# A planned fp32 decoder kernel on one core: norm weights by rows at the layer boundary, one PSUM tile per transpose group, two buffers of transposed probabilities, and a planner with other durations

## The chip, the core and the metric

The kernel runs on one core of one Trainium2 chip. The number that counts is the device time of one execution in microseconds (us). The engines of the core are PE (TensorE, matrix products; its weight loads are listed apart as PEld), DVE (VectorE), ACT (ScalarE), POOL (GpSimd) and SP (SyncE, which here only issues DMAs). Each engine takes its instructions in the order in which they were written, so an instruction that waits holds back all that stand behind it on that engine. SBUF is the on-chip memory, and PSUM is the memory that PE writes and that DVE and ACT read.

## The reference, cut to what is computed

Two layers, 256 tokens, 1024 channels, then a final norm. Each layer reads one normalised input through one wide projection, runs three token mixers on it (a: block attention, which for 256 tokens is plain causal attention; b: attention over the keys that a small indexer selects, 64 for each query; c: attention with a running sum of forget gates as bias), gates each, projects each, merges them by sigmoid gates and adds an output projection to the residual.

```python
def hybrid_layer(x, gain, w_in, f_bias, w_branch, w_out):
    h = rms_norm(x, gain)                      # x * rsqrt(mean(x*x) + eps) * gain
    proj = einsum('bsd,de->bse', h, w_in)      # q,k,v,gate of a, b, c; indexer; forget; merge logits
    oa = moba_attention(rope(qa), rope(ka), va) * silu(ga)
    ob = dsa_attention(rope(qb), rope(kb), vb, rope(qi), rope(ki), wi) * silu(gb)
    log_f = log_sigmoid(f_logit + f_bias)
    oc = forgetting_attention(qc, kc, vc, log_f) * silu(gc)
    y = einsum('nbsw,nwd->bsnd', stack([oa, ob, oc]), w_branch)
    merged = sum(sigmoid(merge_logit) * y, axis=2)
    return x + einsum('bsd,de->bse', merged, w_out)

def reference(x, ...):
    for layer in range(2): x = hybrid_layer(x, ...)
    return rms_norm(x, final_gain)
```

## The kernel before

**Numbers.** Everything is float32. Each operand of a product is split into a high part that PE takes exactly and a low part, the rest (`wh`, `wl` for weights, `hTh`, `hTl` for the normalised input, and so on), and each product is made of three matmuls: high by high, high by low, low by high. A weight goes a fixed way: a DMA brings a piece into one of three `raw` buffers (L373), ACT copies its high part into `wh` (L381), DVE subtracts it and writes `wl` (L385), PE multiplies with both (L429). There are 190 such pieces, and six buffers each of `wh` and `wl`.

**Order.** The Python code writes no instruction directly. It lists operations in a `Plan`: each has the engines that may do it with an assumed duration, what it reads and writes, and a key (a due position, counted in matmul units). `Plan.run` then repeats one step: among the operations that are ready it works out how early each could start by the assumed durations, takes the engine that could start first, and on it the operation of the lowest key among those that can start at that earliest moment. So the assumed durations and keys decide, when the program is built, where each instruction stands in each engine's fixed order, and for some operations which engine does them. On the chip the engines keep these orders and wait for one another by semaphores. `MARGIN` and the like are extra lags that the planner leaves between an operation and a matmul that needs it.

**Units.** A layer's work goes in this order: values of mixer a; the unit `kwf` (the indexer's keys, with the forget logits); the indexer's queries and mixer a, with some merge logits between; mixer c, with merges between; mixer b, with merges between; the rest of the merges; the output projection. In a mixer each pair of heads has projections for queries, gates and keys (units of DVE `ql`, `kl`, rotary steps on DVE and POOL, L488 to L491), scores on PE (L613, 2 heads into a PSUM tile `d`), softmax (DVE L687, ACT L691, DVE L694, then a normalising multiply on DVE L701 or ACT L698), transposes of the probabilities (PE L624), their split (ACT `pth` L716, DVE `ptl` L717, one buffer each), products with the values (PE L729 to L732, in this order the two with `pth`, then the two with `ptl`), and the gate (ACT L745, DVE L747, then a multiply by `g` on POOL L752 or DVE L753). The merge of a branch ends in an add to `acc` (DVE L932 or POOL L933).

**The places around the change.**
- Start and layer boundary use one function, `norm_to_hT`, once per token tile of 128: a sum of squares per half of the channels (ACT L499, at the start also DVE L501), mean (DVE L505), power (POOL L507), a scale by it (ACT L516 for one half, DVE L519 for the other), eight PE transposes (L537) into two `d` tiles, and for each of the eight 128-channel blocks an ACT copy times the gain (`hTh`, L544) and a DVE operation for the rest (`hTl`, L551). The gain lies in `gT`, a channel to a partition, for both layers.
- The forget chain hangs on `wf_cols`: fz (DVE L808 to L816, nine small operations), running sum (PE L822 to L824), its copies (DVE L827, L828), a transposed copy written to DRAM (`drow`, L837) and read back to all partitions (`brow`, L839, two DMAs), from which mixer c makes its bias `fb` (DVE L672). It is listed right behind `kwf`.
- The indexer's selection: eight rounds of MAX8 (L890) and MATCH_REPLACE8 (L891) on DVE, then the mask `selb` (L894, L896). Mixer b needs it.
- Each `d` tile counts in the planner as two banks (`Buf.banks`), so that ACT may work on one half and DVE on the other.
- The merged rows are transposed by token tile (PE L941), both tiles into one `d`, and split (ACT L946, DVE L947).
- At the end of the last layer the final gain is loaded by rows into `acc[:, 0]`, which is free by then.

Of the kernel before, what the change touches and what calls it, by code (L numbers as in the profile page):

```python
# [109 lines left out]

class Plan:
# [38 lines left out]
    def run(self, slack):  # L150
# [4 lines left out]
        while ready:  # L155
# [84 lines left out]
def t_pool(n):  # L240
    return 250.0 + 2.2 * n
# [7 lines left out]
def hybrid_trunk(ctx, tc, x, norm_gain, w_in, forget_bias, w_branch, w_out, final_gain, consts, out):  # L249
# [51 lines left out]
    gT = pool.tile([128, L, KC], F32, name="gT")  # L301
# [8 lines left out]
    pts = [pool.tile([128, 2, 384], F32R, name=f"pt{p}") for p in "hl"]  # L310
# [20 lines left out]
    k_id, k_rope, k_gT, k_cst, k_fb, k_wf, k_widx, k_lf, k_cs, k_csT, k_main = (Tok() for _ in range(11))  # L331
# [18 lines left out]
    plan.tag("pth", pts[:1])  # L350
    plan.tag("ptl", pts[1:])
# [12 lines left out]
    def piece(key, ckey, ap, cshape, sel, shape, k):  # L364
# [21 lines left out]
        act(hi, a * b, False, [c], [p[0]], k - SPLIT_LEAD, f"hi {key}", 18.0)  # L386
        dve(lo, a * b, [c, p[0]], [p[1]], k - SPLIT_LEAD, f"lo {key}", port=True)
# [123 lines left out]
    def scaled(i, src, t, reads, key):  # L511

        r = small[:, t, 3:4]
        o = tmp6[:, i * HD:(i + 1) * HD]
        if i == 0:
            act(lambda: ACT.activation(o, src, AF.Copy, scale=r), HD, False, reads + [k_ss[t][2]], [k_tmp[i]], key,  # L516
                "norm", 93.0)
        else:
            dve(lambda: DVE.tensor_scalar(o, src, r, None, op0=ALU.mult), HD, reads + [k_ss[t][2]], [k_tmp[i]], key,  # L519
                "norm", t_dve2(HD) + 61.0)  # L520
        return o

    def norm_to_hT(l, t, key):
        for i in range(2):
            sum_sq(t, i, key, l == 0)
        rstd(t, key)
        for i in range(2):
            scaled(i, xs[t][:, i * HD:(i + 1) * HD], t, [k_x[t][i]], key)
        dd = [Buf("d"), Buf("d")]
        for b in range(4):  # L530
            ps, at = Tok(), [dd[b // 2], dd[b // 2].banks[b % 2]]
            at_cols = lambda k, d=dd[b // 2], b=b: T(d)[:, b % 2 * 512 + k * 128:b % 2 * 512 + (k + 1) * 128]

# [5 lines left out]
            for k in range(2):
                c = b * 2 + k  # L540
                sl = (slice(None), c, slice(t * 128, (t + 1) * 128))
                src = lambda at_cols=at_cols, k=k: at_cols(k)
                g = gT[:, l, c:c + 1]
                act(lambda sl=sl, src=src, g=g: ACT.activation(hTh[sl], src(), AF.Copy, scale=g), 128, True,  # L544
                    [ps, k_gT], [k_hT[0][t][c]], key, "hT", 93.0, touch=at)
            for k in range(2):
                c = b * 2 + k
                sl = (slice(None), c, slice(t * 128, (t + 1) * 128))
                src = lambda at_cols=at_cols, k=k: at_cols(k)
                g = gT[:, l, c:c + 1]  # L550
                dve(lambda sl=sl, src=src, g=g: DVE.scalar_tensor_tensor(  # L551
                    hTl[sl], src(), g, hTh[sl].bitcast(F32), op0=ALU.mult, op1=ALU.subtract), 128,
                    [ps, k_gT, k_hT[0][t][c]], [k_hT[1][t][c]], key, "hT", t_dve(128) + 61.0, touch=at)
# [74 lines left out]
    class Pair:  # L628
# [49 lines left out]
        def softmax(self, d, key):  # L678
            bs = [self.bias(h, key) for h in range(2)]
            es, ke = [], []  # L680
            for h in range(2):
# [12 lines left out]
                dve(lambda st=st: DVE.reciprocal(T(st)[:, 4:6], T(st)[:, 2:4]), 2, [], kt, key, "recip", 75.0, touch=[st])  # L694
# [13 lines left out]
        def values(self, ps, key):  # L708
# [25 lines left out]
            pe(av, 696.0, kv + [ph, pl] + [t for h in kp for t in h], [o], key, "av", MARGIN)  # L734
# [4 lines left out]
        def gated(self):  # L739
# [9 lines left out]
            def gate():  # L749
# [3 lines left out]
                     ("DVE", t_dve(S), lambda: DVE.tensor_tensor(*gate(), op=ALU.mult))],  # L753
# [29 lines left out]
    def wf_cols(l, key):  # L783
# [15 lines left out]
        dve(pre, 0, [ps, k_fb], [k_lf], key, "lf", 300.0)  # L799

# [348 lines left out]
```

## Time and profile before

Times of the kernel: 599.23, 599.30 and 599.63 us, median 599.3. The profiled execution took 598.98 us, and its span from the first to the last instruction is 597.1 us.

| engine | busy us | share of the span | instructions |
|---|---|---|---|
| PE | 587.2 | 98% | 4332 |
| DVE | 516.8 | 87% | 1164 |
| ACT | 387.0 | 65% | 736 |
| POOL | 100.2 | 17% | 110 |

The page has the time of each engine, a strip of 40 slices, the DMA queues, the chain of work that ended last, and groups of instructions by line and operation. Further views of the trace are used below: PE's waits, grouped by the line waited for; windows, which give each engine's busy time in stretches of the span; groups kept apart by shape; and the timeline, one row for each run of like instructions: start, duration, engine, line, operation, result and operands, and in brackets the idle time of that engine just before, with what ended it. PE pipelines its matmuls, so rows overlap: what a matmul costs is the distance from its start to the next start.

### The profile page before, as it was taken

How to read it: one execution, taken by the hardware profiler on the slowest of the kernel's cores; microseconds unless marked ns; L12 is line 12 of the kernel's file. 1: busy time of each engine (PE TensorE's matmuls, PEld its weight loads, DVE VectorE, ACT ScalarE, POOL GpSimd, SP SyncE). 2: the span in 40 equal slices, each digit the busy share in tenths (PEclk: the TensorE clock that was granted, in tenths of full speed). 3: DMA queues.
4: the chain of work that ended last, by engine and by line, in shares of the span. 5: the costliest groups of instructions: out<-in, count | busy, mean ns of one | idle time of the engine just before them, and what ended most of it. 6: DMA issues, size and time to landing. Idle time of an engine off the chain costs nothing.

```text
span 597.1 us, 11359 instructions
## 1 busy us (share of the span) xinstructions
PE 587.2 (98%) x4332; PEld 538.2 (90%) x4332; DVE 516.8 (87%) x1164; ACT 387.0 (65%) x736; POOL 100.2 (17%) x110
## 2 busy tenths in 40 slices
PE   8999999999999999999999999999999999999995
PEld 7989998989998999888889899898999899998885
DVE  6799999877898989978588999997869898998773
ACT  5767539585677757774487754676748785758441
POOL 1241040200000334200004221320000023440001
PEclk9999999999999999999999999999999999999999
DMA  8849546546464554474546747464574464447411
GB/s 289 278 145 349 176 131 228 181 136 213 140 212 143 155 199 142 145 264 155 164 141 212 249 149 240 142 212 143 176 246 143 141 212 142 143 144 271 150 35 72
DMA packets 75831, 107.59 MB, mean 180 GB/s; under 512 B 4208, under 2 KB 45440, under 8 KB 75776
## 3 DMA queue, kind: packets, MB, share of 16 engines
q1 hardware_dynamic: 75488, 106.47, 54.4%
q8 instruction: 34, 0.56, 0.4%
q10 hardware_dynamic: 288, 0.39, 0.2%
q14 instruction: 21, 0.17, 0.1%
HBM read 105.79 MB, written 1.06 MB: 179 GB/s over the span
## 4 chain that ended last, share of the span: by engine, by line
PE 85%; DVE 10%; issue 2%; ACT 1%; DMA 1%; POOL 0%; POOLq 0%; DVEq 0%
PE proj L429 74%; PE d L613 4%; DVE wl L385 3%; PE proj L1027 2%; PE d L624 2%; PE o L732 1%; PE o L729 1%; DVE isc L891 1%; DVE t L890 1%; PE o L731 1%; PE d L941 1%; DVE rsh L488 1%; DMA x<-in_x_dram 1%; PE o L730 0%; ACT wh L381 0%
## 5 line engine op out<-in xcount | busy, mean ns | idle before, releaser
L385 DVE TENSOR_TENSOR wl<-raw,wh 128x1024 fp32r<-128x1024 f32 (+1 forms) x190 | 235.1, 1250 | 26.3 <-ACT wh L381 23.2
L381 ACT ACTIVATE wh<-raw 128x1024 fp32r<-128x1024 f32 (+1 forms) x190 | 198.2, 1055 | 74.7 <-PE proj L429 37.1
L429 PE MATMUL proj<-hTh,wh 128*128 128x256 f32 (+1 forms) x656 | 155.6, 276 | 0.0
L429 PE MATMUL proj<-hTl,wh 128*128 128x256 f32 (+1 forms) x656 | 154.9, 275 | 0.0
L429 PEld LDWEIGHTS proj<-hTh,wh 128*128 128x128 f32 (+1 forms) x656 | 125.2, 191 | 0.6
L429 PEld LDWEIGHTS proj<-hTl,wh 128*128 128x128 f32 (+1 forms) x656 | 125.2, 191 | 0.3
L429 PE MATMUL proj<-wh,hTh 128*128 128x512 f32 x272 | 105.1, 386 | 0.0
L429 PE MATMUL proj<-wh,hTl 128*128 128x512 f32 x272 | 103.3, 380 | 0.2 <-DVE hTl L551 0.2
L429 PE MATMUL proj<-hTh,wl 128*128 128x256 f32 (+1 forms) x656 | 100.4, 276 | 0.0
L429 PEld LDWEIGHTS proj<-hTh,wl 128*128 128x128 f32 (+1 forms) x656 | 86.2, 191 | 0.2
L429 PE MATMUL proj<-wl,hTh 128*128 128x512 f32 x272 | 81.0, 379 | 0.3 <-DVE wl L385 0.3
L489 POOL TENSOR_TENSOR rsh<-rsh,cst 128x256 f32<-128x256 f32 (+1 forms) x42 | 38.4, 915 | 165.9 <-DVE rsh L488 164.3
L429 PEld LDWEIGHTS proj<-wl,hTh 128*128 128x128 f32 x272 | 51.3, 189 | 7.9 <-DVE wl L385 0.7
L429 PEld LDWEIGHTS proj<-wh,hTl 128*128 128x128 f32 x272 | 51.5, 189 | 7.5 <-DVE hTl L551 1.2
L429 PEld LDWEIGHTS proj<-wh,hTh 128*128 128x128 f32 x272 | 51.4, 189 | 7.5
L691 ACT ACTIVATE e<-e,st 128x128 f32<-128x128 f32 x96 | 42.4, 443 | 22.8 <-DVE st L687 22.5
L491 POOL TENSOR_TENSOR rr<-rr,rsh 128x256 f32<-128x256 f32 (+1 forms) x42 | 41.5, 989 | 12.6 <-DVE rr L490 8.8
L752 POOL TENSOR_TENSOR ot<-ot,g 128x256 f32<-128x256 f32 x10 | 8.1, 814 | 200.6 <-DVE ot L747 129.1
L429 PE MATMUL proj<-wh,v 128*128 128x512 f32 (+1 forms) x144 | 34.0, 359 | 0.0
L429 PEld LDWEIGHTS proj<-wh,v 128*128 128x128 f32 x144 | 25.1, 190 | 2.8
L429 PE MATMUL proj<-wh,og0h 128*128 128x512 f32 x64 | 25.0, 391 | 0.0
L717 DVE TENSOR_TENSOR ptl<-d,pth 128x768 fp32r<-128x768 f32 x24 | 22.9, 953 | 2.2 <-ACT pth L716 1.9
(193 smaller groups left out, 926.8 us busy)
## 6 DMA issues: line engine op xcount, KB each, us to landing
raw<-in_w_in_dram SPq DMA_DIRECT2D x74, 1024.0 KB, 5.2
raw<-in_w_branch_dram SPq DMA_DIRECT2D x12, 1024.0 KB, 5.1
raw<-in_w_out_dram SPq DMA_DIRECT2D x8, 1024.0 KB, 5.1
brow<-drow SPq DMA_DIRECT2D x4, 512.0 KB, 6.6
raw<-in_w_in_dram SPq DMA_DIRECT2D x3, 512.0 KB, 6.2
x<-in_x_dram SPq DMA_DIRECT2D x4, 256.0 KB, 5.5
raw<-in_w_in_dram SPq DMA_DIRECT2D x2, 320.0 KB, 6.2
out_dram<-tmp SPq DMA_DIRECT2D x2, 320.0 KB, 2.5
```

The source lines that it names most:

```text
L381: ACT.activation(p[0].v, sel(c.v), AF.Copy)
L385: DVE.tensor_tensor(p[1].v, sel(c.v), p[0].v.bitcast(F32), op=ALU.subtract)
L429: PE.matmul(o(), a(), b(), start=first and i == 0, stop=last and i == n - 1)
L488: dve(lambda: DVE.stream_shuffle(T(sh)[:np_], a(), SWAP), S, [ps], [sh], key, "rope", t_dve(S) + 6.0)
L489: gps(lambda: POOL.tensor_tensor(T(sh)[:np_], T(sh)[:np_], s[:np_], op=ALU.mult), S, [k_rope], [sh], key, "rope")
L491: gps(lambda: POOL.tensor_tensor(T(r)[:np_], T(r)[:np_], T(sh)[:np_], op=ALU.add), S, [sh], [r], key, "rope")
L613: PE.matmul(T(d)[:, c:c + n].rearrange("p (b a) -> p b a", a=2), st[r, sl], turns(mv[r, :n]), start=i == 0, stop=i == 2, skip_group_check= ...
L624: PE.matmul(T(d)[:, u * 512 + j * 64:u * 512 + j * 64 + 64], e[r], ident[r, r], is_transpose=True, start=True, stop=True, skip_group_check ...
L691: act(lambda t=t, a=a, n=n, e=e, st=st: ACT.activation(T(e)[:, a:a + n], T(e)[:, a:a + n], AF.Exp, bias=T(st)[:, t:t + 1], scale=-1.0, acc ...
L717: dve(lambda src=src, dst=dst: DVE.tensor_tensor(dst(pl), src(), dst(ph).bitcast(F32), op=ALU.subtract), 128 * n, [ps, k[0]], k[1:], key, ...
L752: plan.op([("POOL", t_pool(S), lambda: POOL.tensor_tensor(*gate(), op=ALU.mult)), ("DVE", t_dve(S), lambda: DVE.tensor_tensor(*gate(), op= ...
L1027: PE.matmul(T(ps[t]).rearrange("p (b a) -> p b a", a=2), h(2 * i + x, t), turns(v3(w)[:, x]), start=left[t][0] == 23, stop=left[t][0] == 0)
```

## The change

The parts, with the names of the diff:

1. **Start.** `norm_to_hT` is now `first_hT` for layer 0. Its transposes go into four PSUM tiles for each token tile, two transposes to a tile, by `GROUPS` (for the first token tile `d`, `proj`, `d`, `proj`), in place of halves of two `d` tiles. `gT` holds the gain of layer 0 alone. The second token tile's input comes by one DMA.
2. **Boundary.** The new `norm_to_hT` has the gain of layer 1 loaded by rows into `acc[:, 0]` ("next gain", 512 KB, as the final gain was already). One DVE operation per half multiplies x by the power and the gain; four PE transposes go to one `d` tile; ACT copies 512 wide and DVE subtracts 512 wide, where there were four operations each. The sum of squares may be on DVE here too. Its DVE and POOL operations have a `rush` of 400 ns: the planner may take them though something else could start up to 400 ns sooner. Their keys are 10 and 8 units ahead instead of 2.
3. **PSUM tiles.** A `d` tile is one bank to the planner (`[Bank()] * 2`), and the merged rows have a `d` tile for each token tile.
4. **Probabilities.** Two buffers each of `pth` and `ptl` (`pt0h`, `pt1h`, `pt0l`, `pt1l`).
5. **Forget chain.** `wf_cols` stops after the first two small operations; the rest is a function `forget`, which is listed after the units of mixer a, with a later key.
6. **Durations.** The planner's assumed times: POOL 320 instead of 250 ns as the fixed part, split copies +42 and +54 ns, `split_to` 90 and 110, a gate's split 100, the gate on DVE +80, reciprocal 91; the lag ahead of the products with the values 600 instead of `MARGIN` (200), ahead of the half-row products 300.
7. ACT's first table is asked for at the start by a Tanh on `half`.

```diff
-        self.no, self.last, self.banks = None, None, [Bank(), Bank()]
+        self.no, self.last, self.banks = None, None, [Bank()] * 2
...
-            e = min(best, key=best.get)
+            e = min(cand, key=lambda c: c[0] - c[3].rush)[4][0]
             lim = best[e] + slack.get(e, 0.0)
-            t, _, _, o, w = min((c for c in cand if c[4][0] == e and c[0] <= lim), key=lambda c: (c[1], c[2]))
+            t, _, _, o, w = min((c for c in cand if c[4][0] == e and c[0] <= lim + c[3].rush), key=lambda c: (c[1], c[2]))
...
 def t_pool(n):
-    return 250.0 + 2.2 * n
+    return 320.0 + 2.2 * n
...
-    pts = [pool.tile([128, 2, 384], F32R, name=f"pt{p}") for p in "hl"]
+    pts = [pool.tile([128, 2, 384], F32R, name=f"pt{i}{p}") for p in "hl" for i in range(2)]
...
+    def norm_to_hT(l, t, key):
+        a = len(plan.ops)
+        for i in range(2):
+            sum_sq(t, i, key, True)
+        r = rstd(t, key)
+        for i in range(2):
+            c = slice(i * HD, (i + 1) * HD)
+            x, o = xs[t][:, c], tmp6[:, c]
+            d = Buf("d")
+            dve(lambda x=x, o=o, c=c: DVE.scalar_tensor_tensor(o, x, r, acc[:, 0, c], op0=ALU.mult, op1=ALU.mult), HD,
+                [k_x[t][i], k_ss[t][2], k_fg, k_acc[0][0], k_acc[1][0]], [k_tmp[i]], key, "norm")
+            at, kt, ks4 = [d, d.banks[0]], Tok(), slice(4 * i, 4 * i + 4)
...
+            act(lambda h=h, src=src: ACT.activation(h, src(), AF.Copy), HD, True, [kt], k_hT[0][t][ks4], key, "hT", touch=at)
+            dve(lambda h=h, lo=lo, src=src: DVE.tensor_tensor(lo, src(), h.bitcast(F32), op=ALU.subtract), HD,
+                [kt] + k_hT[0][t][ks4], k_hT[1][t][ks4], key, "hT", t_dve(HD) + 10.0, touch=at)
+        for o in plan.ops[a:]:
+            if {w[0] for w in o.ways} <= {"DVE", "POOL"}:
+                o.rush = RUSH
...
-            pe(av, 696.0, kv + [ph, pl] + [t for h in kp for t in h], [o], key, "av", MARGIN)
+            pe(av, 696.0, kv + [ph, pl] + [t for h in kp for t in h], [o], key, "av", 600.0)
...
-                     ("DVE", t_dve(S), lambda: DVE.tensor_tensor(*gate(), op=ALU.mult))],
+                     ("DVE", t_dve(S) + 80.0, lambda: DVE.tensor_tensor(*gate(), op=ALU.mult))],
...
+        return lambda k: forget(l, k, z, na, e, u, c, lf)
...
         for f in between(first, m_of(l, 0, gates) + m_of(l, 2, gates, HC)):
             f()
+        sums(units[0])
...
+        g = final_gain.rearrange("(o d) -> o d", o=1) if last else norm_gain[l + 1:l + 2]
+        dma(lambda g=g: nc.sync.dma_start(acc[:, 0], g.to_broadcast([128, D])), 512 * D, [],
+            [k_fg] + [t for k in k_acc for t in k], units[0], "next gain")
...
-                    norm_to_hT(l + 1, t, u - 2)
+                    norm_to_hT(l + 1, t, u - NK[t])
```

The orders that come out of it are shown at three places. A row is a source line, an operation, its result and operands with their buffer numbers, and the size of the result.

**First place: DVE behind the first `kwf` unit, layer 0.** Here the forget chain (`fz`, `csum`, `ncs`) meets the weights' low parts `wl`. Before:

```order
L385 TENSOR_TENSOR wl_73<-raw_125,wh_66 128x1024
L488 STREAM_SHUFFLE rsh_127<-proj_162 128x256
L808 TENSOR_SCALAR fz<-fz 128x16
...
L816 SCALAR_TENSOR_TENSOR fz<-fz 128x16
L416 TENSOR_TENSOR ql_89<-rr_129,qh_86 128x256
L416 TENSOR_TENSOR ql_90<-rr_128,qh_87 128x256
L490 TENSOR_TENSOR rr_129<-proj_162,cst 128x256
L385 TENSOR_TENSOR wl_74<-raw_125,wh_67 128x1024
L827 COPY csum<-d_164 128x16
```

After:

```order
L387 TENSOR_TENSOR wl_74<-raw_127,wh_67 128x1024
L387 TENSOR_TENSOR wl_75<-raw_125,wh_68 128x1024
L387 TENSOR_TENSOR wl_70<-raw_125,wh_63 128x1024
L832 TENSOR_SCALAR fz<-fz 128x16
...
L840 SCALAR_TENSOR_TENSOR fz<-fz 128x16
L490 STREAM_SHUFFLE rsh_128<-proj_164 128x256
L418 TENSOR_TENSOR ql_90<-rr_130,qh_87 128x256
```

The nine `fz` operations stood ahead of `wl_74` and stand behind `wl_74`, `wl_75` and `wl_70`; `csum` is gone from here (it is now some 190 rows further on, behind the second pair of `ptl`s).

**Second place: DVE ahead of the first split of transposed probabilities (`ptl`), layer 0, mixer a.** Before:

```order
L385 TENSOR_TENSOR wl_71<-raw_124,wh_64 128x1024
L672 SCALAR_TENSOR_TENSOR fb_149<-brow,ncs,cst 128x128
L385 TENSOR_TENSOR wl_72<-raw_124,wh_65 128x1024
L385 TENSOR_TENSOR wl_73<-raw_125,wh_66 128x1024
L717 TENSOR_TENSOR ptl<-d_164,pth 128x768
L385 TENSOR_TENSOR wl_74<-raw_125,wh_67 128x1024
L672 SCALAR_TENSOR_TENSOR fb_149<-brow,ncs,cst 128x256
L717 TENSOR_TENSOR ptl<-d_163,pth 128x768
```

After:

```order
L418 TENSOR_TENSOR ql_89<-rr_131,qh_86 128x256
L418 TENSOR_TENSOR ql_90<-rr_130,qh_87 128x256
L387 TENSOR_TENSOR wl_75<-raw_125,wh_68 128x1024
L387 TENSOR_TENSOR wl_70<-raw_125,wh_63 128x1024
L737 TENSOR_TENSOR pt0l<-d_166,pt0h 128x768
L737 TENSOR_TENSOR pt1l<-d_165,pt1h 128x768
L387 TENSOR_TENSOR wl_71<-raw_126,wh_64 128x1024
```

The mixer-c biases `fb` are no longer here, and the two `ptl`s follow one another, with a buffer each. Over DVE's whole order up to the first `ptl`, and start aside, the change takes out 3 `wl` (32 to 29), 3 `fb`, `csum` and `ncs`, one MAX8 and two MATCH_REPLACE8, and the four `selb` operations, and adds one pair of normalising multiplies.

**Third place: DVE at the layer boundary, first token tile** (`x_111`, then `x_113`, is its residual). Before:

```order
L1114 TENSOR_TENSOR x_111<-x_111,proj_161 128x512
L505 SCALAR_TENSOR_TENSOR small<-small 128x1
L519 TENSOR_SCALAR tmp_113<-x_111,small 128x512
L385 TENSOR_TENSOR wl_73<-raw_125,wh_66 128x1024
L385 TENSOR_TENSOR wl_74<-raw_125,wh_67 128x1024
L385 TENSOR_TENSOR wl_75<-raw_123,wh_68 128x640
L551 SCALAR_TENSOR_TENSOR hTl<-d_164,gT,hTh 128x128
L1114 TENSOR_TENSOR x_112<-x_112,proj_162 128x512
L551 SCALAR_TENSOR_TENSOR hTl<-d_164,gT,hTh 128x128 x3
```

After:

```order
L1136 TENSOR_TENSOR x_113<-x_113,proj_162 128x512
L503 ISA tmp_115,small<-x_113 128x512
L503 ISA small 128x1
L507 SCALAR_TENSOR_TENSOR small<-small 128x1
L558 SCALAR_TENSOR_TENSOR tmp_115<-x_113,small,acc 128x512 x2
L387 TENSOR_TENSOR wl_73<-raw_127,wh_66 128x1024
L569 TENSOR_TENSOR hTl<-d_166,hTh 128x4x128
L569 TENSOR_TENSOR hTl<-d_165,hTh 128x4x128
L1136 TENSOR_TENSOR x_114<-x_114,proj_163 128x512
```

The sum of squares (L503) and both halves of the scaling (L558) are on DVE now, one `wl` instead of three stands between them and the first `hTl`, and `hTl` is two operations for a token tile.

More of the change, by code (lines that the diff above doesn't have):

```diff
@@ L349, in hybrid_trunk @@
     plan.tag("ql", qs[1])
-    plan.tag("pth", pts[:1])
-    plan.tag("ptl", pts[1:])
+    plan.tag("pth", pts[:2])
+    plan.tag("ptl", pts[2:])
     plan.tag("k", ks)
@@ L509, in rstd @@
         return small[:, t, 3:4]
[L511 to L521, printed above, removed]
@@ L538, in norm_to_hT @@
             pe(tr, 220.0, [k_tmp[b // 2], k_id], [ps], key, "hT", touch=at)
[L539 to L553, printed above, removed]
+            for w in range(2):
+                for k in range(2):
+                    c = b * 2 + k
+                    sl = (slice(None), c, slice(t * 128, (t + 1) * 128))
+                    src = lambda d=d, k=k: T(d)[:, k * 128:(k + 1) * 128]
+                    g = gT[:, c:c + 1]
+                    if w == 0:
+                        act(lambda sl=sl, src=src, g=g: ACT.activation(hTh[sl], src(), AF.Copy, scale=g), 128, True,
+                            [ps, k_gT], [k_hT[0][t][c]], key, "hT", 93.0, touch=at)
+                    else:
+                        dve(lambda sl=sl, src=src, g=g: DVE.scalar_tensor_tensor(
+                            hTl[sl], src(), g, hTh[sl].bitcast(F32), op0=ALU.mult, op1=ALU.subtract), 128,
+                            [ps, k_gT, k_hT[0][t][c]], [k_hT[1][t][c]], key, "hT", t_dve(128) + 61.0, touch=at)
@@ L599, in half_rows @@
         fs, cost, reads, writes, touch = zip(*jobs)
-        pe(go, sum(cost) + SWITCH, [r for x in reads for r in x], [w for x in writes for w in x], key, name, MARGIN,
+        pe(go, sum(cost) + SWITCH, [r for x in reads for r in x], [w for x in writes for w in x], key, name, 300.0,
            touch=[t for x in touch for t in x])
@@ L951, in hybrid_trunk @@
     DVE.memset(ones, 1.0)
-    DVE.memset(half, -0.5)
     warm, spare = plan.tags["d"][0][1], plan.tags["o"][0][1]
@@ L964, in hybrid_trunk @@
         load(xs[0][:, i * HD:(i + 1) * HD], xr[0][:, i * HD:(i + 1) * HD], 512 * HD, [k_x[0][i]], -102 + i, "x0", 950.0)
-    load(gT.rearrange("p l k -> p (l k)"), norm_gain, 8192, [k_gT], -94.9, "gain")
+    load(gT, norm_gain[0].rearrange("(p k) -> p k", k=KC), 8192, [k_gT], -94.9, "gain")
+    DVE.memset(half, -0.5)
+    ACT.activation(csum[:, 0, :1], half, AF.Tanh)
     def identity():
@@ L973, in late_loads @@
     def late_loads():
-        for i in range(2):
-            load(xs[1][:, i * HD:(i + 1) * HD], xr[1][:, i * HD:(i + 1) * HD], 512 * HD, [k_x[1][i]], -90 + i, "x1")
+        load(xs[1], xr[1], 512 * D, k_x[1], -90, "x1")
         load(cst[:, C_ROPE:], consts[:, C_ROPE:], 512 * 1024, [k_rope], -12 + 1.5, "rope")
@@ L1136 @@
     feed = {n: np.ascontiguousarray(inputs[n]) for n in _INS}
-    feed["norm_gain"] = np.ascontiguousarray(feed["norm_gain"].reshape(L * KC, 128).T)
+    gain = feed["norm_gain"].copy()
+    gain[0] = gain[0].reshape(KC, 128).T.reshape(-1)
+    feed["norm_gain"] = gain
     feed["consts"] = shape_constants()
```

69 lines of the change are left out of this document (39 added, 30 removed).

## The prediction

> **What bounds the kernel now.** I read the page first: busy times and the chain that ended last.
>
> ```profile
> PE 587.2 (98%) x4332; PEld 538.2 (90%) x4332; DVE 516.8 (87%) x1164; ACT 387.0 (65%) x736; POOL 100.2 (17%) x110
> PE 85%; DVE 10%; issue 2%; ACT 1%; DMA 1%; POOL 0%; POOLq 0%; DVEq 0%
> ```
>
> PE is busy for all but about 10 us of the span, and the change neither adds nor removes a matmul (it only regroups transposes). So time can come only from PE's waiting, and the chain's 10% of DVE says whom PE waits for. Second, PE's waits, grouped (us in total, times, the longest; left out is the wait ahead of the first matmul):
>
> ```profile
> PE o L731 <- DVE ptl L717: 1.3, 2, 1.0
> ...
> PE proj L429 <- DVE wl L385: 0.3, 1, 0.3
> PE proj L1027 <- DVE hTl L551: 0.3, 1, 0.3
> PE d L613 <- DVE k2l L416: 0.2, 1, 0.2
> PE d L624 <- DVE e L701: 0.2, 1, 0.2
> PE proj L429 <- DVE hTl L551: 0.2, 1, 0.2
> ```
>
> All of them end with DVE; together 2.5 us, of which 0.3 at the start. Third, the windows view says where DVE has no room (stretch, its length, then busy time of PE, PEld, DVE, ACT, POOL, clock, DMA share, GB/s):
>
> ```profile
> 60.00:104.00 44.00, 42.80 (x317) 39.20 (x316) 43.92 (x126) 26.66 (x50) 6.97 (x8) 1.00 0.55 177
> 200.00:270.00 70.00, 69.97 (x539) 64.48 (x537) 63.92 (x139) 48.99 (x96) 20.27 (x20) 1.00 0.52 173
> 350.00:394.00 44.00, 43.49 (x322) 39.82 (x321) 43.89 (x124) 26.41 (x48) 7.14 (x8) 1.00 0.53 173
> 500.00:570.00 70.00, 69.96 (x500) 63.25 (x500) 62.42 (x132) 48.22 (x92) 16.40 (x16) 1.00 0.51 173
> ```
>
> In mixer a of each layer (60 to 104, 350 to 394) DVE is busy for 43.9 of 44 us and PE misses 1.20 and 0.51 us. In mixer b and the merges (200 to 270, 500 to 570) DVE still has 6.1 and 7.6 us, and PE misses under 0.05. The granted clock is 1.00, so no gain hides there.
>
> **The change part by part.** *Mixer a of layer 0.* The dearest wait, on the timeline:
>
> ```profile
> 97.09 2.36 DVE L385 TENSOR_TENSOR wl<-raw,wh 128x1024 fp32r<-128x1024 f32 x2
> 99.19 0.22 PE L730 MATMUL o<-pth,v 128*128 128x128 f32 x1
> 99.37 0.95 DVE L717 TENSOR_TENSOR ptl<-d,pth 128x768 fp32r<-128x768 f32 x1
> 100.37 0.27 PE L731 MATMUL o<-ptl,v 128*64 128x128 f32 x1 [0.96 <-DVE ptl L717]
> 100.70 0.22 PE L730 MATMUL o<-pth,v 128*128 128x128 f32 x1
> 100.76 0.22 PE L731 MATMUL o<-ptl,v 128*64 128x128 f32 x1
> ```
>
> From L730 to L731 PE takes 1.18 us where an undisturbed pair (the last two rows) takes 0.06: a loss of 1.12. DVE had been in its queue's weights until 99.37. Ahead of that `ptl` the change takes from DVE (order, second place): 3 `wl` at 1.25, 3 `fb`, `csum`, `ncs`, some rounds of the selection and the four `selb`, and adds one pair of normalising multiplies. The durations of the dearer groups:
>
> ```profile
> L385 DVE TENSOR_TENSOR wl<-raw,wh 128x1024 fp32r<-128x1024 f32 x188 | 233.6, 1255 | 26.3 <-ACT wh L381 23.2 <-PE o L732 0.8 <-PE proj L429 0.4
> L672 DVE SCALAR_TENSOR_TENSOR fb<-brow,ncs,cst 128x128 f32<-128x128 f32 x16 | 5.5, 343 | 0.0
> L753 DVE TENSOR_TENSOR ot<-ot,g 128x256 f32<-128x256 f32 x14 | 6.9, 490 | 0.2
> L932 DVE TENSOR_TENSOR acc<-acc,mth 128x512 f32<-128x512 f32 x12 | 8.3, 688 | 0.3
> L752 POOL TENSOR_TENSOR ot<-ot,g 128x256 f32<-128x256 f32 x10 | 8.1, 814 | 200.6 <-DVE ot L747 129.1
> ```
>
> That is 3 x 1.25 = 3.8 for `wl` and at least 3 x 0.34 = 1.0 for `fb`; four `selb` operations and three of the selection on like sizes, at some 0.3 each or more, are 2: near 7 us, against under 1 for the pair added. PE's order loses a dozen matmuls and the running sum ahead of the place, under 3 us at 0.22 each. DVE so gains 3 us or more on PE where it was late by 1.1. I take the loss to shrink from 1.12 to 0.25 (gain 0.87; bounds 0 if DVE's new room is eaten by waiting for ACT, 1.12), and the wait on `k2l` by half (gain 0.2, bounds -0.4 and 0.4).
>
> *The forget chain.* Its nine operations stood ahead of the `wl` that PE wanted:
>
> ```profile
> 34.82 0.15 DVE L808 TENSOR_SCALAR fz<-fz 128x16 f32<-128x16 f32 x1
> 37.09 0.17 DVE L816 SCALAR_TENSOR_TENSOR fz<-fz 128x16 f32<-128x16 f32 x1
> 38.26 1.21 DVE L385 TENSOR_TENSOR wl<-raw,wh 128x1024 fp32r<-128x1024 f32 x1
> 38.83 0.38 PE L429 MATMUL proj<-wh,hTl 128*128 128x512 f32 x1
> 39.53 0.70 PE L429 MATMUL proj<-wl,hTh 128*128 128x512 f32 x2 [0.32 <-DVE wl L385]
> ```
>
> They fill 2.4 us of DVE; the next matmul of a pair starts 0.22 later as a rule, here 0.70: a loss of 0.48. After the change three `wl` stand ahead of the chain (order, first place), so this loss goes (gain 0.48; bounds 0 and 0.48). The `brow` loads move with it, to SP behind mixer a; they take 6.6 us to land, 4 of them in all:
>
> ```profile
> brow<-drow SPq DMA_DIRECT2D x4, 512.0 KB, 6.6
> ```
>
> Mixer c's first `fb` stands behind that mixer's second gate `g` in DVE's order, which follows PE and not DVE's own speed; I cost the move at nothing, hidden by PE's matmuls up to that gate (bounds 0 and, should nothing cover it, 6.6 a layer; the third rival holds its chance). If that cover is gone, DVE waits at `fb` with `wl` and `k` behind it, and PE after DVE's lead is used up.
>
> *Two buffers of probabilities and the lag of 600.* Mixer b's first pair in layer 0 loses a little too:
>
> ```profile
> 230.51 0.22 PE L730 MATMUL o<-pth,v 128*128 128x128 f32 x1
> 230.76 0.27 PE L731 MATMUL o<-ptl,v 128*64 128x128 f32 x1
> ```
>
> 0.25 against 0.06, so 0.19, and I count the same in layer 1. Gain 0.4 with bounds 0 and 0.4.
>
> *Layer 1, mixer a.* There the views show a wait on `e` of 0.2 and the shorter `ptl` wait, 1.3 - 1.0 = 0.3; the rows above lose about 0.16 more than their brackets, so 0.8 together. DVE's room grows less surely there, as the order differs: gain 0.5, bounds -0.3 and 0.8.
>
> *Boundary.* Rows of DVE, ACT and PE:
>
> ```profile
> 298.40 3.26 DVE L385 TENSOR_TENSOR wl<-raw,wh 128x1024 fp32r<-128x1024 f32 x3
> 301.57 0.34 DVE L551 SCALAR_TENSOR_TENSOR hTl<-d,gT,hTh 128x128 fp32r<-128x128 f32 x1
> 300.20 2.15 ACT L544 ACTIVATE hTh<-d,gT 128x128 fp32r<-128x128 f32 x8
> 302.29 0.38 PE L429 MATMUL proj<-wh,hTh 128*128 128x512 f32 x1
> 302.83 0.48 PE L429 MATMUL proj<-wh,hTl 128*128 128x512 f32 x1 [0.15 <-DVE hTl L551]
> ```
>
> PE waits for `hTl`, which DVE begins only after three `wl`: 0.54 from 302.29 to 302.83 instead of 0.22, and the waits view has another 0.2 for it. Now one `wl` stands there (order, third place), and `hTl` is two operations of about 0.69 (the nearest row, L932, is as wide and has two operands) instead of eight of 0.34. Two sums of squares and the other half of the scaling, also 512 wide, are new on DVE, 2 us by the same row at most; two `wl`, 2.5 us, moved behind them. So DVE reaches `hTl` no later, and needs 1.4 where it needed more than 2. Gain 0.42 (0.1 left; bounds -0.5, if the longer DVE chain makes the transposes late, and 0.52). The 512 KB gain load stands on SP ahead of one `raw` load; by the `brow` row it lands within 6.6 us, and I cost it at nothing.
>
> *Start.* ACT's `hTh` and DVE's `hTl` took turns on one tile, and PE waited 0.30 for it:
>
> ```profile
> 9.61 0.48 PE L1027 MATMUL proj<-wh,hTl 128*128 128x512 f32 x1 [0.30 <-DVE hTl L551]
> ```
>
> The tile per group lets ACT run ahead, but ACT also takes a 1024-wide `wh` copy that DVE had, and DVE a sum of squares; the second token tile's chain is no shorter, and its transposes change PE's mode twice more. I take a loss of 0.25 (bounds: the 0.30 gained, and about 0.6 lost, one 512-wide operation in the chain).
>
> *POOL's work to DVE.* Ten gates at 0.49 and four `acc` adds at 0.69 come to DVE: 7.7 us. POOL had them at 0.81 and longer. They fall mostly where DVE has room (by POOL's rows 2 gates and 2 adds, 2.4 us, into each of the stretches with 6.1 and 7.6 us of it). I take 0.3 us of new small waits (bounds 0 and the rival below). Whether DVE gets something back because POOL is silent depends on rows like these:
>
> ```profile
> 32.87 1.67 DVE L385 TENSOR_TENSOR wl<-raw,wh 128x1024 fp32r<-128x1024 f32 x1
> 219.02 1.22 DVE L385 TENSOR_TENSOR wl<-raw,wh 128x1024 fp32r<-128x1024 f32 x1
> 219.18 2.20 POOL L933 TENSOR_TENSOR acc<-acc,mth 128x512 f32<-128x512 f32 x1 [4.61 <-DVE mth L930]
> ```
>
> At 219 a `wl` runs beside a POOL add and takes its usual 1.22: DVE lost nothing there, so I count nothing back. The Trainium skill (SBUF — State Buffer, section "Who interferes with whom") states that a DVE instruction with two SBUF inputs contends with a GpSimd instruction that reads SBUF, under an exclusive lock whose loser blocks fully. With that rule the trace agrees, and it says that whoever starts first wins: at 219 DVE started first and the add took 2.20, at 32.87 the `wl` took 1.67. By the rule the ten gates could give DVE back at most their 8.1 us, which is worth something only where PE waits for DVE; the sum goes without.
>
> **Sum.** 0.87 + 0.2 + 0.48 + 0.4 + 0.5 + 0.42 = 2.87 gained, 0.25 + 0.3 lost: about 2.3 net, most of it in five places. The tail after the last matmul isn't touched. From the profiled execution, 598.98 - 2.3 = 596.7; the median of the runs is 599.3, 0.3 above it, so **597.0** as a median.
>
> **The rivals.**
> - *The waits only move* (0.20). DVE stays at 43.9 of 44 in mixer a, since it follows ACT's `wh`, and what it gained ahead of the first `ptl` is lost at `k2l` and `e`. Then only the forget chain, the pairs and half the boundary are left, 0.48 + 0.4 + 0.2, less 0.55: 598.8. For it: DVE was the bound in the whole stretch, not in one place. Against it: over 6 us leave the queue and 1.1 was missing. The change then does little of what it says.
> - *Everything goes well* (0.13). All waits between 28 and 570 us go: 2.2 by the view, and with the 0.16 each that brackets miss and the two small pairs about 4.0; the start gains too. 599.3 - 4.3 = 595.0. A reason would be that POOL's ten gates at 0.81 had held DVE up, as the `wl` at 32.87 was, so that up to 8 us come back to DVE. The row at 219.02 speaks against.
> - *DVE becomes the bound in mixer b* (0.15), the slower side. The 14 operations that were POOL's stand in DVE's queue ahead of softmax and `wl`, where PE waits as soon as DVE's lead is used up. Each then costs its own time: if the 2 gates and 2 adds of each late stretch do, 2 x 2.4 = 4.7 us. 599.3 - 2.3 + 4.7 = 601.7. It decides once DVE's busy share there goes above about 95%: it is 91% and 89%, with 2.4 of 70 us added 95% and 93%. A late `brow` would act alike in mixer c.
>
> **How the numbers follow.** My forecast has 0.52, the rivals 0.20, 0.13 and 0.15. What a measurement of this kernel can tell from no change is about 0.2%, 1.2 us. Faster: 0.52 less a little that ends within 0.2%, plus 0.13: 0.64. Same: 0.20 and that little: 0.22. Slower: 0.14. The range: the lower end is the best case, 595.0; the upper goes past no change to the milder half of the third rival, 600.4, which leaves under 2 in 10 outside. The likeliest case alone spans 595.8 to 598.0.
>
> **What would show it.** In the profile after: no PE wait on `wl` near 38 us; the first L730 to L731 distance under 0.4 us; DVE under 42 of 44 us in mixer a; PE's L429 matmuls on `hTl` at the boundary 0.22 apart; PE's wait list under 1.2 us without its first line; DVE busy near 524 us and POOL near 85. It is wrong if PE gets waits on `ptl`, `e` or `wl` between 200 and 270 us, on `fb` in mixer c, or if the second token tile at the start or boundary is late.

## The result, and the profile after

The changed kernel takes 595.45 us in the median of 6 runs (594.43 to 597.55), the kernel before 599.38 (599.23 to 599.63): a ratio of 0.9938, with a 95% interval of 0.9928 to 0.9948. That is 3.9 us faster, where 2.3 was forecast. The profiled execution, 594.43 us with a span of 592.6, is the quickest of the six, which matters below. In a later run of the same kernel (e0) the profiled execution took 1013.2 us at a mean granted clock of 0.557; it is left out, so that run has times to compare and no profile.

The page and PE's waits of the changed kernel, the lines that answer to those of before:

```profile
PE 584.6 (99%) x4332; PEld 538.8 (91%) x4332; DVE 524.4 (88%) x1169; ACT 382.5 (65%) x722; POOL 89.8 (15%) x96
PE 85%; DVE 12%; issue 1%; ACT 1%; POOL 0%; POOLq 0%; DVEq 0%
PE d L978 <- DVE half L989: 1.1, 1, 1.1
PE o L749 <- DVE ot L767: 0.9, 2, 0.6
```

DVE has more to do than before (524.4 against 516.8 us) and holds PE up less. All five kinds of wait that PE had behind the start are gone. One is new, twice: on `o`, the one PSUM tile of the products with the values. The windows:

```profile
60.00:104.00 44.00, 43.73 (x331) 40.35 (x330) 43.91 (x125) 28.59 (x52) 7.94 (x8) 1.00 0.55 179
200.00:270.00 70.00, 70.00 (x527) 64.38 (x526) 65.96 (x144) 46.77 (x92) 14.33 (x14) 1.00 0.53 174
350.00:394.00 44.00, 43.41 (x335) 40.41 (x334) 41.22 (x118) 28.16 (x52) 8.96 (x10) 1.00 0.57 189
500.00:570.00 70.00, 70.00 (x494) 63.28 (x493) 64.78 (x136) 46.15 (x90) 8.95 (x9) 1.00 0.52 171
```

PE misses 0.27 us of the first stretch (1.20 before), 0.59 of the third (0.51), and nothing of mixer b, though DVE is at 94% and 93% there. (The stretches are cut at the same times as before; the work in them has moved up by 1 to 4 us.) The new wait, on the timeline of layer 0:

```profile
97.82 0.28 PE L431 MATMUL proj<-hTl,wh 128*128 128x256 f32 x1
98.37 0.35 PE L749 MATMUL o<-pt1h,v 128*128 128x256 f32 x1 [0.27 <-DVE ot L767]
95.11 2.35 DVE L387 TENSOR_TENSOR wl<-raw,wh 128x1024 fp32r<-128x1024 f32 x2
97.37 0.85 DVE L767 SCALAR_TENSOR_TENSOR ot<-o,ot 64x256 f32<-64x256 f32 x2
```

With two buffers the second pair's probabilities are ready early, so PE comes to its product while DVE, behind two `wl`, is still reading the first pair's `o`. From 97.82 to 98.37 is 0.55 where 0.11 is usual: 0.44 lost, and 0.75 at the same place of layer 1. The boundary, where PE lost 0.52 before, runs at 0.22 from start to start (298.38, 298.59, 298.81, 299.02):

```profile
296.13 1.22 DVE L387 TENSOR_TENSOR wl<-raw,wh 128x1024 fp32r<-128x1024 f32 x1
297.47 1.29 DVE L569 TENSOR_TENSOR hTl<-d,hTh 128x512 fp32r<-128x512 f32 x2
298.38 0.38 PE L431 MATMUL proj<-wh,hTh 128*128 128x512 f32 x1
298.59 0.38 PE L431 MATMUL proj<-wh,hTl 128*128 128x512 f32 x1
```

The start is 1.19 us shorter in these two profiles: the first matmul of `kwf`, before (first row) and after:

```profile
22.46 0.27 PE L429 MATMUL proj<-hTh,wh 128*80 128x256 f32 x1
21.27 0.27 PE L431 MATMUL proj<-hTh,wh 128*80 128x256 f32 x1
```

So of the 4.5 us between the spans 1.2 lie at the start. Behind it, by distances from start to start in the two profiles, 4.07 us of waits went (0.48 at the forget chain, 1.13 and 0.45 in mixer a, 0.40 at the pairs, 0.52 at the boundary, 1.09 in layer 1's mixer a), 1.19 came at `o`, and 0.4 are left in distances too small to name.

### The profile page after: what moved, and what is told of

Its sections match the earlier page's. It is cut to its first block, busy times and chain, and to the rows that moved or that the text cites. A ratio compares the mean times of both kernels' runs of the same rounds, so it can differ in the third digit from the quotient of the medians.

```text
span 592.6 us, 11315 instructions
## 1 busy us (share of the span) xinstructions
PE 584.6 (99%) x4332; PEld 538.8 (91%) x4332; DVE 524.4 (88%) x1169; ACT 382.5 (65%) x722; POOL 89.8 (15%) x96
## 4 chain that ended last, share of the span: by engine, by line
PE 85%; DVE 12%; issue 1%; ACT 1%; POOL 0%; POOLq 0%; DVEq 0%
PE proj L431 73%; DVE wl L387 5%; PE d L633 4%; PE proj L1050 2%; DVE isc L915 2%; PE d L644 2%; DVE t L914 1%; PE d L978 1%; PE o L749 1%; PE o L752 1%; DVE e L707 1%; PE d L965 1%; DVE rsh L490 1%; PE o L750 0%; PE o L751 0%
## 5 line engine op out<-in xcount | busy, mean ns | idle before, releaser
L387 DVE TENSOR_TENSOR wl<-raw,wh 128x1024 fp32r<-128x1024 f32 (+1 forms) x190 | 239.3, 1276 | 21.1 <-ACT wh L383 18.3
L491 POOL TENSOR_TENSOR rsh<-rsh,cst 128x256 f32<-128x256 f32 (+1 forms) x42 | 33.4, 795 | 350.0 <-DVE rsh L490 350.0
L493 POOL TENSOR_TENSOR rr<-rr,rsh 128x256 f32<-128x256 f32 (+1 forms) x42 | 52.0, 1237 | 15.1 <-DVE rr L492 12.5
L431 PE MATMUL proj<-wh,og0l 128*128 128x512 f32 x64 | 24.3, 379 | 0.0
L767 DVE SCALAR_TENSOR_TENSOR ot<-o,ot 64x256 f32<-64x256 f32 x48 | 19.9, 414 | 1.3 <-ACT ot L765 0.9
```

Of the source, the lines that this page charges most:

```text
L387: DVE.tensor_tensor(p[1].v, sel(c.v), p[0].v.bitcast(F32), op=ALU.subtract)
L431: PE.matmul(o(), a(), b(), start=first and i == 0, stop=last and i == n - 1)
L491: gps(lambda: POOL.tensor_tensor(T(sh)[:np_], T(sh)[:np_], s[:np_], op=ALU.mult), S, [k_rope], [sh], key, "rope")
L493: gps(lambda: POOL.tensor_tensor(T(r)[:np_], T(r)[:np_], T(sh)[:np_], op=ALU.add), S, [sh], [r], key, "rope")
L767: dve(lambda r=r, h=h: DVE.scalar_tensor_tensor(T(t)[r], T(o)[:64, h * S:(h + 1) * S], 0.5, T(t)[r], op0=ALU.mult, op1=ALU.add), S, [o], [ ...
```

## The experiments

Theory A at the outset: each part takes away the wait that it was made for, and the gains add. Theory B: the planner's durations and lags make the gain. All medians, each beside its own runs of the kernel before (599.4 to 599.5). The last column is from the one profiled execution of each: the time from the first matmul of `kwf` to the end, which leaves the start out. It is 574.7 for the kernel before and 571.4 for the changed one.

| run | what it is | median us | ratio to before, 95% interval | behind the start, us |
|---|---|---|---|---|
| e0_again | changed kernel | 595.22 | 0.9931 (0.9915 to 0.9948) | no profile |
| e1_start_only | before, with the new start | 599.04 | 0.9993 (0.9984 to 1.0002) | 575.2 |
| e2_chain_back | changed, forget chain as before | 596.02 | 0.9934 (0.9918 to 0.9951) | 573.2 |
| e3_one_pt | changed, one buffer of probabilities | 596.58 | 0.9951 (0.9936 to 0.9966) | 572.5 |
| e5_old_boundary | changed, boundary as before | 597.87 | 0.9974 (0.9962 to 0.9986) | 574.2 |
| e6_gates_pool | changed, gates on POOL | 599.26 | 1.0000 (0.9991 to 1.0010) | 575.5 |
| e4_old_durations | changed, part 6 as before | 599.51 | 1.0000 (0.9990 to 1.0009) | 575.5 |
| e10_lags_back | changed, lags alone as before | 596.13 | 0.9947 (0.9931 to 0.9962) | 572.4 |
| e11_costs_back | changed, durations alone as before | 599.42 | 0.9998 (0.9988 to 1.0007) | 575.4 |
| e12_before_durations | before, with part 6 alone | 600.31 | 1.0013 (1.0004 to 1.0023) | 576.6 |
| e8_power_first | changed, one wait more at the start | 595.93 | 0.9941 (0.9926 to 0.9956) | 571.8 |
| e7_o_lag | changed, a lag of 900 behind `o` | 593.94 | 0.9908 (0.9890 to 0.9925) | 570.4 |

The changed kernel's own interval is 0.9928 to 0.9948. By their intervals e5, e6, e4 and e11 are slower than it and e7 is faster; e2, e3, e10 and e8 lie too near to be told from it by time alone, and what is said of them rests on their profiles. One profile can be off by half a microsecond: e1 has the waits of before behind the start, and 575.2.

**e1_start_only.** The new start in the kernel before:

```diff
-        norm_to_hT(0, t, -50 + t)
+        first_hT(t, -50 + t)
```

> The kernel before with nothing but the new start (a PSUM tile per transpose group, one load for the second token tile, the table asked for early). In the profiles the first matmul of kwf moved from 22.46 us to 21.27. Theory A (each part removes its own waits, and they add): the time falls by that 1.2 us, to about 598.2 (597.9 to 598.5); the waits behind 28 us stay as they were before, ptl's 1.0 and hTl's 0.2 among them. Theory B (the planner's room makes the gain, the start is a by-product of other orders): within 0.3 us of before.

Measured 599.04 us, 0.4 faster, with an interval from 1.0 faster to 0.1 slower; the waits behind 28 us stayed as they were (ptl 1.0, hTl 0.2). By the median both theories missed: the start gives something, and not the 1.2 of the two profiles. The interval still leaves room for theory B. In this profile `kwf` begins at 22.78, no earlier than before. Why is seen on POOL, DVE and PE of this run (rows 1 to 3) and of the changed kernel (4 to 6):

```profile
12.37 1.22 DVE L1055 TENSOR_TENSOR wl<-raw,wh 128x1024 fp32r<-128x1024 f32 x1
12.39 1.61 POOL L507 TENSOR_TENSOR small<-small,half 128x1 f32<-128x1 f32 x1 [6.23 <-DVE small L505]
14.81 0.66 PE L543 MATMUL d<-cst,tmp 128*128 128x128 f32 x4 [0.84 <-ACT tmp L532]
11.94 0.55 POOL L509 TENSOR_TENSOR small<-small,half 128x1 f32<-128x1 f32 x1 [6.14 <-DVE small L507]
12.14 1.23 DVE L1042 TENSOR_TENSOR wl<-raw,wh 128x1024 fp32r<-128x1024 f32 x1 [0.29 <-ACT wh L1039]
13.30 0.66 PE L533 MATMUL d<-cst,tmp 128*128 128x128 f32 x4
```

POOL's power for the second token tile takes 0.55 us where it begins ahead of DVE's `wl`, and 1.61 where that begins 0.02 us sooner; the norm and PE's transposes hang on it. All profiles agree: in the six in which the `wl` began first, by 0.02 to 0.16 us, the power ended 0.41 us behind the end of that `wl` (in e1 at 14.00 against 13.59), and in the others it took 0.55 or 0.56. In the changed kernel's profile the `wl` happened to wait 0.29 us for its `wh`, and ACT, which makes it, waited 0.25 for the load. Without that wait the `wl` would have begun at 11.85, ahead of the power. So a load that lands later could make an earlier start; that follows from these rows, and no run tests it.

**e2_chain_back.** The chain listed at once, in the changed kernel:

```diff
-        sums = wf_cols(l, u + 1)
+        wf_cols(l, u + 1)(u + 1)
...
-        sums(units[0])
```

> The changed kernel with the forget chain listed right behind kwf again. Theory A: the wait on wl near 38 us (0.48) comes back, and part of the ptl wait (0 to 0.9), in layer 1 a like part: 0.5 to 2 us over the changed kernel. Theory B: under 0.3 us, since margins and durations feed PE anyway.

Measured 596.02, 0.6 over the changed kernel in the median, which is not clear of noise (the ratios, 0.9934 and 0.9938, are the same). Its profile is 1.8 us longer behind the start, within theory A's range; it was the slowest of the four runs. And the wait is another one than before. PE stands once, for `wl`, near 91 us, not near 38 (timeline of PE and DVE):

```profile
90.11 2.34 DVE L387 TENSOR_TENSOR wl<-raw,wh 128x1024 fp32r<-128x1024 f32 x2
91.37 0.70 PE L431 MATMUL proj<-wl,hTh 128*128 128x512 f32 x2 [1.57 <-DVE wl L387]
```

**e3_one_pt.** One buffer each:

```diff
-    plan.tag("pth", pts[:2])
-    plan.tag("ptl", pts[2:])
+    plan.tag("pth", pts[:1])
+    plan.tag("ptl", pts[1:])
```

> The changed kernel with one buffer each of pth and ptl, as before. The changed kernel's only two mid-kernel waits are new: PE's second product with the values waits for DVE's read of the one PSUM tile o that both pairs share (0.44 and 0.75 us more than usual). If the second buffer brought that wait forward, those two go here and ptl waits of up to 1 us each come in their place: within 1 us of the changed kernel either way. If the second buffer carries much of the gain: over 1.5 us slower.

Measured 596.58, 1.1 over, and 1.1 over in the profile behind the start. The two waits on `o` went, as expected; the `ptl` waits did not come. PE waits at the end of mixer b instead, on the last pair's gated output, 1.02 us there and 0.89 in layer 1:

```profile
265.99 2.35 DVE L387 TENSOR_TENSOR wl<-raw,wh 128x1024 fp32r<-128x1024 f32 x2
268.26 0.42 DVE L418 TENSOR_TENSOR og0l<-ot,og0h 128x256 fp32r<-128x256 f32 x1
268.73 0.48 PE L431 MATMUL proj<-wh,og0l 128*128 128x512 f32 x1 [0.86 <-DVE og0l L418]
```

**e5_old_boundary.** The old `norm_to_hT` for layer 1, gain by columns:

```diff
-                    norm_to_hT(l + 1, t, u - NK[t])
+                    norm_to_hT(l + 1, t, u - 2)
```

> The changed kernel with the old layer boundary (gain by columns from gT, eight copies 128 wide, two halves of a d tile, keys 2 ahead, no rush). Theory A: the boundary's 0.52 us comes back, 0.3 to 0.8 us over the changed kernel, with a PE wait on hTl. Theory B (moves elsewhere hide it): no PE wait on hTl and under 0.3 us.

Measured 597.87, 2.4 over the changed kernel: theory A's place and sign, at three times the upper end of its size. PE waits for `hTl` for both token tiles, 0.99 and 0.94 us by distances. For the first tile DVE comes from the same three `wl` as before; for the second it waited 0.34 us itself, for ACT's `hTh`, so that one has another cause:

```profile
295.90 3.26 DVE L387 TENSOR_TENSOR wl<-raw,wh 128x1024 fp32r<-128x1024 f32 x3
300.27 0.48 PE L431 MATMUL proj<-wh,hTl 128*128 128x512 f32 x1 [0.83 <-DVE hTl L589]
307.60 0.48 PE L431 MATMUL proj<-wh,hTl 128*128 128x512 f32 x1 [0.68 <-DVE hTl L589]
```

**e0_again** and **e8_power_first.** The changed kernel once more, and with one wait more at the start:

```diff
-                    512 * n, [kr] + ths, tls, HI_KEY[i] + 0.5, ...
+                    512 * n, [kr] + ths + ([k_ss[1][2]] if i == 2 else []), tls, HI_KEY[i] + 0.5, ...
```

> The changed kernel again, beside the next three, since its runs spread over 3 us (594.4 to 597.6) where the kernel before spreads over 0.4 to 1.3. Theory C: the spread is made at the start. POOL's power for the second token tile takes 0.55 us where it starts before DVE's next wl and about 1.55 where that wl starts first, and which comes first hangs on when the loads land. Then a profile here either has the 0.55 and kwf's first matmul near 21.3, or the 1.5 and kwf at 22 or later, and its time is about 1 us longer in the second case; the waits behind 28 us are the same two (0.44 and 0.75). Rival: the waits in mid-kernel vary from run to run.

> The changed kernel with one wait more: DVE's wl of the third piece at the start also waits for the second token tile's power, so that POOL always starts first. Theory C: the power takes 0.55 in every run, kwf's first matmul stays between 21.2 and 22.0, the runs lie within 1 us of one another and the median falls by 0.3 to 1.0 us against the changed kernel. Rival (the power is not what varies): the spread stays, and the median moves by under 0.3 us or rises, as the wl is up to 0.9 us later.

e0's three runs took 595.08 to 595.78; without a profile it tells the theories apart in nothing. e8's lie within 0.32 us (595.79 to 596.11) with the power at 0.55, as theory C has it, but the median didn't fall, and `kwf` began at 22.52: PE waited 0.5 us for the first token tile's `hTh` and 0.24 for the delayed `wl`. The power's length is one thing that moves the start and not the only one; the other is when it begins. In all ten other profiles with the new start, `kwf` begins 8.78 us after the power for the second token tile has ended (e1: 14.00 and 22.78, the changed kernel: 12.49 and 21.27), and in e8, whose delayed `wl` cost PE 0.24, after 9.16. The power begins between 11.94 and 13.22 us, and takes 0.55 or 1.47 to 1.61.

**e6_gates_pool.** Gates on POOL alone, in the changed kernel:

```diff
-            plan.op([("POOL", t_pool(S), ...), ("DVE", t_dve(S) + 80.0, ...)],
+            plan.op([("POOL", t_pool(S), ...)],
```

> The changed kernel with all 24 gate multiplies on POOL alone. DVE loses 24 x 0.49 = 11.8 us of busy time, and gets back what POOL's 24 x 0.81 us block. Theory of the prediction (POOL's gates fall where DVE's operands are in PSUM, or POOL is the one that waits, so a gate on DVE costs its full time, but in room that DVE has): DVE busy near 513 us, and the time within 0.7 us of the changed kernel. Rival (gates on DVE were a loss): over 1 us faster. Second rival (a gate on POOL is later by 0.3 us and more, and ACT's split behind it is late): over 1 us slower, with PE waits on og.

Measured 599.26, 3.8 slower: the second rival. PE's waits and DVE's `wl`, in e6 (first three rows) and in the changed kernel (last):

```profile
PE proj L431 <- ACT og0h L417: 1.7, 2, 0.9
PE proj L431 <- DVE og0l L418: 0.9, 2, 0.5
L387 DVE TENSOR_TENSOR wl<-raw,wh 128x1024 fp32r<-128x1024 f32 x188 | 243.2, 1310 | 30.3 <-ACT wh L383 28.4 <-ACT tmp L881 0.7
L387 DVE TENSOR_TENSOR wl<-raw,wh 128x1024 fp32r<-128x1024 f32 x188 | 237.6, 1281 | 21.1 <-ACT wh L383 18.3 <-ACT tmp L882 0.7
```

The wait stands at the end of mixer b again: the last gate takes 0.80 us on POOL instead of 0.48 on DVE, and ACT's and DVE's split behind it are late, 1.02 + 0.74 us by distances in layer 0 and 1.01 + 0.74 in layer 1. DVE was rid of 11.8 us of gates, yet its busy time fell only from 524.4 to 521.8: its 188 `wl` took 5.6 us more. Seven of them overlap a gate on POOL; these took 1.61 us in the mean instead of 1.22, which is 2.7 us. The rest lies in `wl` beside POOL's rotary steps, which fall elsewhere in this order.

**e4_old_durations, e10_lags_back, e11_costs_back.** Part 6 as before in whole, and in its halves:

```diff
-    return 320.0 + 2.2 * n
+    return 250.0 + 2.2 * n
...
-        act(hi, a * b, False, [c], [p[0]], k - SPLIT_LEAD, f"hi {key}", 42.0)
+        act(hi, a * b, False, [c], [p[0]], k - SPLIT_LEAD, f"hi {key}", 18.0)
...
-        ea, ed = (0.0, 10.0) if ps else (90.0, 110.0)
+        ea, ed = (0.0, 10.0) if ps else (72.0, 26.0)
```

These and the other durations (e11), the two lags (e10), or both (e4).

> The changed kernel with all the planner's durations and lags of before (part 6: POOL 250, split copies without their 42 and 54, 72 and 26, 16, recip 75, lags of 200). Theory A: the waits that the lags of 600 took away come back (two of 0.2), some ptl wait with them: 0.4 to 1.5 us slower than the changed kernel. Theory B (the durations are what feeds PE): over 2 us slower, with waits in many places.

> The changed kernel with the two lags alone as before (200 ahead of the products with the values in place of 600, 200 ahead of a group of scores or transposes in place of 300), the durations new. With all of part 6 as before the kernel took 599.5, so part 6 carries the gain. If the lags carry it: 598 to 599.5, with ptl, k and e waits. If the durations do: within 0.7 us of the changed kernel.

> The changed kernel with the durations alone as before, the lags new (600 and 300): the complement of the run with the lags as before. If the durations carry the gain: 598 to 599.5, with waits of PE in several places where the order believes a copy is done sooner than it is. If the lags do: within 0.7 us of the changed kernel. If both halves stay near 595.5 the two hide each other's lack; if both are near 599 each is needed.

Undone alone, the lags cost 0.7 us (596.13, not clear of noise), the durations 4.0 (599.42), both 4.1 (599.51): without the durations the other parts together gain nothing. PE then waits in several places. One of the three dearest in e11, layer 1's scores, with DVE and POOL beside it:

```profile
372.50 0.87 DVE L920 TENSOR_TENSOR selb<-selb,cst 128x256 f32<-128x256 f32 x1
373.16 0.79 POOL L493 TENSOR_TENSOR rr<-rr,rsh 128x256 f32<-128x256 f32 x1
373.29 0.95 DVE L418 TENSOR_TENSOR k3l<-rr,k3h 128x256 fp32r<-128x256 f32 x1
374.29 0.38 PE L633 MATMUL d<-k3l,qh 64*128 64x256 f32 x2 [1.09 <-DVE k3l L418]
```

The `k3l` split takes 0.95 beside POOL, where the changed kernel has it at 0.48 with POOL silent. The old durations count 0.36 us for it (`t_dve(256)` and 26 ns), the new ones 0.44. PE was sent to the scores when `k3l` was to be done; but neither figure covers the 0.95, so this wait isn't explained by that one figure. The other two, 1.23 and 1.28 us ahead of products with the values, are waits on `o` again, now in mixer b. The second of them, in layer 1:

```profile
525.08 0.89 DVE L767 SCALAR_TENSOR_TENSOR ot<-o,ot 64x256 f32<-64x256 f32 x2
526.12 0.35 PE L749 MATMUL o<-pt1h,v 128*128 128x256 f32 x1 [1.11 <-ACT wh L383]
```

The bracket names ACT's `wh`, but the product does not read it; what it needs is that DVE has read `o`, which ended at 525.97.

**e12_before_durations.** Part 6 alone, in the kernel before.

> The kernel before with part 6 alone (new durations and lags), nothing else. If part 6 carries the gain by itself: 595.5 to 597. If it only does with the other parts (two buffers, chain, boundary): 598 to 600, with the boundary's hTl wait (0.5) and a ptl or og wait left.

Measured 600.31, 0.8 slower than before, just beyond the range that was expected: the durations do nothing good alone. Its waits of PE:

```profile
PE proj L429 <- DVE og0l L416: 1.6, 2, 0.9
PE proj L429 <- DVE wl L385: 1.6, 1, 1.6
...
PE proj L429 <- DVE hTl L551: 0.4, 1, 0.4
```

They are those of e3 (og0l; 1.03 and 0.90 us by distances, in e3 1.02 and 0.89), e2 (wl; 1.74, in e2 1.73) and e5 (hTl; 0.94 and another 0.4 at the transposes ahead of it, in e5 1.93). So with the new durations the order has three sore places, and each of the other parts heals one: the second buffer the end of mixer b, the chain's move the `wl` near 91, the new boundary `hTl`. Neither theory says this; the two halves need one another. Not settled is whether the new durations help because they are nearer the truth or because the one order that comes out happens to be a good one: each run draws a single order, and e7 shows that another number of the planner moves the time as well.

**e7_o_lag.** The changed kernel, with the planner told that `o` comes free later:

```diff
-b.end + (1500.0 if b.tag == "raw" else SEM)
+b.end + {"raw": 1500.0, "o": 900.0}.get(b.tag, SEM)
```

> The changed kernel with 900 ns in place of 70 as the planner's lag between the last read of the PSUM tile o and its next use, so that PE's second products with the values are planned some 12 matmuls later. Theory: the two new waits on DVE's read of o (0.44 and 0.75 us in the changed kernel's profile) go, and nothing else moves much: 0.6 to 1.2 us faster than the changed kernel, near 594.5. Rival (any change of the planner's numbers moves waits to other places, since the order behind that point is drawn anew): the two waits go and others come, within 0.5 us or slower.

Measured 593.94 us (593.62 to 594.67), 1.5 faster than the changed kernel, beyond the expected 0.6 to 1.2, and the best of all: 0.9908 of before. The profiles behind the start differ by 1.0, near the 1.19 that stood at `o`; the other half microsecond is not explained. In its list of PE's waits only the start is left:

```profile
PE d L978 <- DVE half L989: 1.1, 1, 1.1
PE d L533 <- ACT tmp L522: 0.8, 1, 0.8
PE proj L1050 <- ACT hTh L542: 0.4, 1, 0.4
```

## Why the prediction was right, and where its steps were not

The sign and the range held: PE's waits behind DVE were what could go, and they went. The size did not: 595.45 lies below the 595.8 to 598.0 of the likeliest case, and nearer to the second rival's 595.0 than to 597.0. That rival had the waits right (all that stood between 28 and 570 us went, and in the profile the start gained), but not its reason, that DVE gets time back from POOL: DVE's `wl` took 237.6 us instead of 233.6. By the prediction's own steps:

- *Mixer a of layer 0* (0.87 and 0.2 forecast). The `ptl` and `k2l` waits went wholly, 1.13 and 0.45. The sign "DVE under 42 of 44 us in mixer a" came in layer 1 (41.22) and not here: DVE has 43.91, and is early all the same. The net is 1.14 where 1.07 was forecast. That this is so near is luck: more went than was forecast, and a wait that no step named took part of it back, the one on `o`, 0.44, which the second buffer brought.
- *Forget chain* (0.48) and *pairs* (0.4): gone in the profile, as forecast. *Boundary* (0.42): 0.52.
- *Layer 1* (0.5): 1.09 went, 0.75 came at `o`: 0.34.
- *New small waits* (0.3 lost): none but `o`, which is counted above.
- *Start* (0.25 lost): the term of the wrong sign. It gained 0.4 by e1 (between 1.0 and -0.1, so it may be nothing), and 1.19 in the profiled execution, which had the 0.55 power and is the quickest run. That the second token tile's chain "is no shorter" left out that its length is settled by which of POOL and DVE begins first.
- *POOL's work to DVE.* That DVE has room for it was right (94% and 93%, PE misses nothing), and the third rival, DVE as the bound in mixer b, did not come: with the gates on POOL (e6) the kernel is slower there. "DVE lost nothing there, so I count nothing back" was read from one row, a `wl` that had begun first. It holds for the kernel before, where only two `wl` overlap a gate and take their usual 1.22 us; in e6's order seven do, at 2.7 us in all. The Trainium skill's rule (SBUF — State Buffer, "Who interferes with whom": the engine that starts second blocks) agrees with e1's rows, where the power ends 0.41 us behind the `wl`.

The sum came to 2.3 and 3.9 was measured; the start's term makes up 0.65 of the difference by e1, and the waits behind it about 0.7 by the profiles (2.88 net of `o` and 0.4 of small ones, against 2.87 - 0.3 = 2.57); some 0.2 stay open. What the working took for granted, that each edit earns its own wait, was not tested by the sum and does not hold: with the old durations the same edits earn nothing (e11), and the durations alone lose 0.8 (e12). The prediction got by without it, because it compared the two final orders and not the edits.

Open: which of the several durations matters (they were put back together only), why any of them does, and what makes the power at the start begin up to 1.3 us later in one profile than in another.

## What to carry to other kernels

In a planned kernel an edit's worth is that of the whole order: parts 1 to 5 and 7 together gave nothing beside the old durations (e4) and 4.9 us beside the new ones (e12 to the changed kernel), so read the final order for each engine, and test by undoing and by doing alone. Look at assumed durations as at an edit of their own: here they decided whether the others were worth anything. A split that takes longer than its figure leaves PE waiting at its product, as `k3l` did. When a second buffer takes a wait away, look for the next single buffer on the same path: here a lag behind `o` gave another 1.5 us, of which the profiles place 1.0.

## What the runs showed of the hardware

POOL and DVE hold one another up by who begins first, and 0.02 us can decide: the one-column power took 0.55 us, or 1.61 where a `wl` had begun 0.02 us sooner. The power then ended 0.41 us behind the `wl`, in all six profiles in which the `wl` came first. In those `kwf` began at 22.46 to 23.05, in five with 0.55 at 21.3 to 22.0, and in two with 0.55 (e7 and e8) at 22.5, because there the power began later, at 13.22 and 12.80.
